# First transfers, products without a reader, row maxima on another engine and a 25th weight slot in a transformer layer with 32 experts

## The chip, the cores and the metric

The kernel runs on one core of one Trainium2 chip. The metric is the device time of one execution in microseconds (us): the median of the runs that are shown. The core has TensorE (PE in the profile; its weight loads are PEld), VectorE (DVE), ScalarE (ACT), GpSimd (POOL) and SyncE (SP), which here only issues transfers. The transfers themselves are carried by 16 DMA engines.

## What is computed

One transformer layer over 256 tokens of width 1024, in float32: attention in three branches (NSA), a gated recurrence (HGRN2), a merge, and 32 experts of which each token takes two.

```python
h = rmsnorm(x, attn_norm[layer])
proj = h @ w_in[layer]
...
mixed = (gate_nsa * (o_nsa.astype(x.dtype) @ w_br_nsa[layer]) +
         gate_hg * (o_hg @ w_br_hg[layer]))
x = x + mixed @ w_out[layer]
x = x + hier_moe(rmsnorm(x, ffn_norm[layer]), w_grp[layer], b_grp[layer], w_rtr[layer], b_rtr[layer],
                 w_gate[layer], w_up[layer], w_down[layer])
...
for e in range(N_EXPERTS):
    hid = jax.nn.silu(t @ w_gate[e]) * (t @ w_up[e])
    out = out + combine[:, e:e + 1] * (hid @ w_down[e]).astype(f32)
```

The expert weights are 32 x 6 pieces of 1 MB; the other weights are 30 blocks of about 1 MB.

## The kernel before

**The front** runs through the 30 blocks of `FRONT` in order: f0, f1, q0, q1, c0, ... m00, ... n1, and last o00, o10, o01, o11 (the product with `w_out`). `load_front` brings a block from HBM into a slot `raw`, on SP's queue. `split_part` (L273, L277) makes two parts of it: ACT writes `whi`, a copy in the reduced format fp32r, and DVE writes `wlo`, what is left. `three` (L410, L412, L413) then multiplies: four products with `whi`, and pairs of one with `wlo` and one with the low part of the other operand; twelve products are a group, four groups a block. For the first blocks the other operand is x^T, scaled by `attn_norm`, split by ACT (L369) and DVE (L371) into `hh_` and `hl_`. The side work of attention and recurrence runs between the groups.

**The slots.** Everything of 8 KB in a partition comes out of one pool of `WSLOTS` slots: raw blocks, `whi`, `wlo`, x, the merged activations `mh` (high parts) and `ml` (low parts), `h2T`, and the expert pieces `we`. A tile takes the slot that comes free first, and what fills it waits until the last reader of the slot's former content is done. `load_expert` (L308, L318) issues the expert pieces, in a fixed order and on SP's queue too: some during the front, by the table `EARLY` (a block's name and how many pieces behind its load), the others behind the front. SP issues in order, and has eight transfers under way at most.

**The routing** stands between o11 and the experts. PE makes the logits (L1024); `route(0)` and `route(1)` choose, for tokens 0 to 127 and 128 to 255, two experts each on DVE, down to a mask `mk` (L1055); `place` counts places with a product `ppos` (L1065) and DVE turns it into `mst` (L1068); `select_tile` makes the 0/1 matrix `lm` out of it (L1094); `gather_tile` gathers the tokens by products `pga` (L1103), which DVE scales into `xe` (L1113). Then the eight quads of four experts begin: `pg` and `pu` (L1207), then `py` (L1261). `residual` (L1121) puts x into the banks `acc`, to which the experts' output is added.

```python
    routed = route(0)
    ...
    with after(i):
        i = residual([0])
    ...
    i = placed[0]
    with after(i):
        i = gather_tile(0, 0, 0)
    i = place(1, i)
```

`after(i)` sets the order on an engine: what stands under it is issued behind i.

## Time and profile before

| | us |
|---|---|
| median of 3 runs | 694.04 |
| lowest, highest | 693.96, 695.82 |
| profiled execution, its own time | 695.66 |
| its span, first to last instruction | 693.9 |

The span is that of the profiled execution, and all times of rows count from its start. The front lies at 0 to 235, the routing at 235 to 247.6, the experts at 247.6 to 680, and the last sums and the store behind them. A view by windows lists, for each stretch, the busy time of each engine, the granted clock of TensorE as a share of 2.4 GHz, the busy share of the DMA engines and what they moved.

### The profile page before, as it was taken

The page shows a single profiled execution, that of the slowest core. Times are in us where ns is not written, and L with a number is a line of the kernel's source. Part 1 is how long each engine was busy: PE and PEld are TensorE (multiplying, and loading weights), DVE is VectorE, ACT ScalarE, POOL GpSimd, SP SyncE. Part 2 cuts the span into 40 slices and gives each one's busy share as a digit, 9 for nine tenths or more (in the row PEclk, how much of TensorE's full clock was granted, in tenths as well). Part 3 has the DMA queues.
Part 4 walks back from the last instruction along what each step waited for, and adds up shares of the span by engine and source line. Part 5 has one row for each costly group of instructions (what it writes and reads, how often), then busy time and mean ns, then how long its engine had stood idle before and what let it go on. Part 6 is the DMA issues. An engine that isn't in the chain of part 4 may idle for free. (4 is left out here: it accounts for less than half of the span.)

```text
span 693.9 us, 8708 instructions
## 1 busy us (share of the span) xinstructions
PE 569.3 (82%) x3628; PEld 318.0 (46%) x3628; DVE 211.4 (30%) x422; ACT 145.4 (21%) x231; POOL 37.3 (5%) x54
## 2 busy tenths in 40 slices
PE   5999999999999999988669668776865977795654
PEld 5988878887897754242123114221411421321111
DVE  5786656667557422121011002200200210110012
ACT  5433548474364210100000000000000000000002
POOL 0423302001000100000000000000000000000001
PEclk9999999999999989999899989988999897999896
DMA  8961533856646989999999999999999999999992
GB/s 321 418 241 65 179 122 148 334 192 232 255 177 248 376 340 421 421 422 419 423 419 422 422 420 421 421 422 420 422 419 422 420 421 422 421 422 419 408 360 89
DMA packets 39931, 238.84 MB, mean 344 GB/s; under 512 B 4176, under 2 KB 8784, under 8 KB 12752
## 3 DMA queue, kind: packets, MB, share of 16 engines
q1 hardware_dynamic: 39456, 237.70, 84.8%
q8 instruction: 30, 0.49, 0.3%
q10 hardware_dynamic: 432, 0.54, 0.2%
q14 instruction: 13, 0.11, 0.0%
HBM read 237.17 MB, written 1.05 MB: 343 GB/s over the span
## 5 line engine op out<-in xcount | busy, mean ns | idle before, releaser
L1207 PE MATMUL pu<-we,xe 128*32 128x512 f32 x512 | 99.2, 719 | 43.4 <-DMA we<-in_w_up 39.8
L1207 PE MATMUL pg<-we,xe 128*32 128x512 f32 x512 | 92.7, 669 | 34.8 <-DMA we<-in_w_gate 34.8
L1261 PE MATMUL py<-we,hT 128*32 128x512 f32 x448 | 74.3, 596 | 8.0 <-DMA we<-in_w_down 8.0
L1231 DVE SCALAR_TENSOR_TENSOR h<-pu,wv,h 128x512 f32<-128x512 f32 x8 | 8.7, 1089 | 234.0 <-PE pu L1207 234.0
L1207 PEld LDWEIGHTS pu<-we,xe 128*32 128x32 f32 x512 | 22.0, 127 | 116.1 <-DMA we<-in_w_up 70.1
L277 DVE TENSOR_TENSOR wlo<-raw,whi 128x2048 fp32r<-128x2048 f32 (+3 forms) x34 | 67.6, 1995 | 19.1 <-ACT whi L273 19.0
L1243 ACT ACTIVATE ys<-py,wv 128x512 fp32r<-128x512 f32 (+1 forms) x17 | 11.3, 663 | 268.0 <-PE py L1261 233.9
L1207 PEld LDWEIGHTS pg<-we,xe 128*32 128x32 f32 x512 | 20.1, 119 | 102.1 <-DMA we<-in_w_gate 64.8
L273 ACT ACTIVATE whi<-raw 128x2048 fp32r<-128x2048 f32 (+3 forms) x34 | 56.1, 1662 | 37.5 <-PE pxs L413 12.5
L412 PE MATMUL pws<-hl__94,whi 128*128 128x256 f32 x192 | 49.6, 289 | 0.0
L413 PE MATMUL pws<-hh__93,wlo 128*128 128x256 f32 x192 | 49.4, 288 | 0.0
L1261 PEld LDWEIGHTS py<-we,hT 128*32 128x32 f32 x448 | 20.4, 109 | 55.7 <-issue 33.7
L410 PE MATMUL pws<-hh__93,whi 128*128 128x256 f32 x192 | 33.9, 300 | 8.3 <-ACT hh__93 L369 8.3
L1244 DVE SCALAR_TENSOR_TENSOR ys<-py,wv,ys 128x512 fp32r<-128x512 f32 (+1 forms) x17 | 12.2, 718 | 89.5 <-ACT ys L1243 88.9
L412 PEld LDWEIGHTS pws<-hl__94,whi 128*128 128x128 f32 x192 | 37.8, 197 | 0.2 <-issue 0.2
L413 PEld LDWEIGHTS pws<-hh__93,wlo 128*128 128x128 f32 x192 | 37.9, 197 | 0.0
L1225 ACT ACTIVATE h<-pg,wv 128x512 f32<-128x512 f32 x8 | 9.2, 1147 | 131.8 <-PE pg L1207 131.8
L1103 PE MATMUL pga<-lm,x 128*128 128x128 f32 x256 | 32.7, 289 | 1.1 <-DVE lm L1094 1.1
L410 PEld LDWEIGHTS pws<-hh__93,whi 128*128 128x128 f32 x192 | 27.6, 197 | 11.2 <-ACT hh__93 L369 8.3
L1103 PEld LDWEIGHTS pga<-lm,x 128*128 128x128 f32 x256 | 31.7, 205 | 2.0 <-DVE lm L1094 2.0
L412 PE MATMUL pxs<-wlo,hh__93 128*128 128x512 f32 (+1 forms) x80 | 29.8, 376 | 0.0
L413 PE MATMUL pxs<-whi,hl__94 128*128 128x512 f32 (+1 forms) x80 | 29.5, 372 | 0.0
(241 smaller groups left out, 644.6 us busy)
## 6 DMA issues: line engine op xcount, KB each, us to landing
we<-in_w_gate SPq DMA_DIRECT2D x64, 1024.0 KB, 19.8
we<-in_w_up SPq DMA_DIRECT2D x64, 1024.0 KB, 19.8
we<-in_w_down SPq DMA_DIRECT2D x60, 1024.0 KB, 19.8
raw<-in_wf SPq DMA_DIRECT2D x27, 1024.0 KB, 4.9
we<-in_w_down SPq DMA_DIRECT2D x8, 512.0 KB, 10.6
raw<-in_wf SPq DMA_DIRECT2D x2, 560.0 KB, 9.9
raw<-in_wf SPq DMA_DIRECT2D x2, 512.0 KB, 6.5
xt__67<-in_xt SPq DMA_DIRECT2D x2, 512.0 KB, 6.9
```

The lines of the kernel that those rows point to most:

```text
L273: i = S.activation(his[n][:, c], raws[n][:, c], AF.Copy)
L277: splits.append((i, V.tensor_tensor(los[n][:, c], raws[n][:, c], his[n][:, c].bitcast(F32), op=OP.subtract)))
L410: PE.matmul(out_, lh, rh, start=start and i == 0, stop=False, skip_group_check=True)
L412: PE.matmul(out_, lh, rl, start=False, stop=False, skip_group_check=True)
L413: last = PE.matmul(out_, ll, rh, start=False, stop=stop and i == n - 1, skip_group_check=True)
L1103: i = PE.matmul(pgs[q, n][:, 128 * k:128 * k + 128], xv[:, tt, 512 * n + 128 * k:512 * n + 128 * k + 128], sel[q][:, tt], start=tt == 0 an ...
L1207: i = PE.matmul(p[32 * e:32 * e + 32], xes[q][:, 4 * hf + k, 32 * e:32 * e + 32], W[4 * q + e, hf][:, k], start=hf == 0 and k == 0, stop=h ...
L1225: S.activation(h, pg.rearrange("p (c j) -> p c j", j=4), AF.Silu, scale=r)
L1231: V.scalar_tensor_tensor(h, pu.rearrange("p (c j) -> p c j", j=4), r, h, op0=OP.mult, op1=OP.mult)
L1243: return (S.activation(hi[:, c], p[:, c], AF.Copy, scale=wv), V.scalar_tensor_tensor(lo[:, c], p[:, c], wv, hi[:, c].bitcast(F32), op0=OP. ...
L1244: V.scalar_tensor_tensor(lo[:, c], p[:, c], wv, hi[:, c].bitcast(F32), op0=OP.mult, op1=OP.subtract))
L1261: PE.matmul(py[n][32 * e:32 * e + 32], hTs[q][:, 2 * kh + j, 32 * e:32 * e + 32], WD[4 * q + e, kh][:, j, 512 * n:512 * n + 512], start=kh ...
```

## The change

- **First transfers.** Block f0 is stored as two halves that are each contiguous in HBM. x^T comes as `xa` (`attn_norm` and the first half), on ACT's queue, and `xb`, on SP's; before, both halves came on SP's queue behind the first half of f0. The vectors `vec` come in one transfer of 168 KB; before, 24 columns came first, on ACT's queue, and the others later.
- **Products without a reader.** 26 products of ones with ones (`WARM`; 128x256, bf16) stand ahead of PE's first product; nothing reads what they give.
- **Shift.** The eight multiplications of row maxima by -0.125 go from POOL (L808) to DVE.
- **Slots.** There are 25. The merged activations are kept by halves (`mT` 0 and 1, high and low part of a half in one slot), `h2T` goes to small tiles, and `EARLY` and the last count of `load_expert` add up to 25 pieces.
- **Routing.** `residual([0])` goes out of the routing into quad 0. In its place stand 16 products that nothing reads (`warm_up`; 128x128, bf16), 14 more behind the first `ppos` and 8 behind the second. The gather of the first 128 tokens is no longer cut by the second `ppos`. In `route(1)` the work of the first tile stands earlier.

```diff
+    blk[FRONT[0]] = blk[FRONT[0]].reshape(128, 2, -1).transpose(1, 0, 2)
...
+    vec = np.concatenate([pm(lb), pm(inp["ffn_norm"]), fin, pm(pos), pm(rt)], 1)
+    xt = rows128(np.ascontiguousarray(np.asarray(inp["x"])[0].T)).reshape(128, -1)
...
+        "xa": con(np.concatenate([an, xt[:, :1024]], 1)), "xb": con(xt[:, 1024:]), "wf": con(wf)[None], "wcmp": con(wc.reshape(128, -1)),
...
-WSLOTS = 24
+WSLOTS = 25
-STB = 1
+WARM = 26
-EARLY = {"h1": 3, "o00": 1, "m21": 1, "m00": 2, "o11": 1, "m01": 2, "m31": 2, "h0": 1, "o01": 1}
+EARLY = {"m20": 1, "h1": 3, "o00": 1, "m21": 1, "m00": 2, "o11": 2, "m01": 2, "m31": 2, "h0": 1, "o01": 2}
...
-    xt_ = slot("xt_")
-    xt8 = xt_.rearrange("p (k t) -> p k t", k=8)
+    xs = [slot(n) for n in ("xa", "xb")]
+    nc.scalar.dma_start(xs[0][:, :1032], xa)
+    an = xs[0][:, :8]
+    xt8 = [t.rearrange("p (k t) -> p k t", k=4) for t in (xs[0][:, 8:1032], xs[1][:, :1024])]
...
-    nc.scalar.dma_start(vc_[:, :24], vec[:, :24])
...
-                nc.sync.dma_start(raws[n][:, o:o + step], bass.AP(tensor=wf.tensor, offset=wf.offset + FOFF[n] + o,
-                                                                  ap=[[w, 128], [1, step]]))
+                nc.sync.dma_start(raws[n][:, o:o + step], bass.AP(tensor=wf.tensor, offset=wf.offset + FOFF[n] + 128 * o,
+                                                                  ap=[[step, 128], [1, step]]))
                 if n == FRONT[0] and o == 0:
-                    for c in range(0, 2048, 1024):
-                        nc.sync.dma_start(xt_[:, c:c + 1024], xt[:, c:c + 1024])
+                    nc.sync.dma_start(xs[1][:, :1024], xb)
...
+    nc.sync.dma_start(vc_, vec)
...
-    xn = slot("xn")
+
+    wz = mid.tile([128, 256], BF16, tag="xe", bufs=1, name="wz")
+    G.memset(wz, 1.0)
+    pw = bank("ns", "pw")
+    for _ in range(WARM):
+        PE.matmul(pw[:, :256], wz[:, :128], wz, start=True, stop=True)
...
-            last_hi = S.activation(hhi[:, k], xt8[:, k], AF.Copy, scale=an[:, k:k + 1])
+            last_hi = S.activation(hhi[:, k], xt8[q][:, k - 4 * q], AF.Copy, scale=an[:, k:k + 1])
         for k in ks:
-            last_lo = V.scalar_tensor_tensor(hlo[:, k], xt8[:, k], an[:, k:k + 1], hhi[:, k].bitcast(F32),
+            last_lo = V.scalar_tensor_tensor(hlo[:, k], xt8[q][:, k - 4 * q], an[:, k:k + 1], hhi[:, k].bitcast(F32),
...
-        G.tensor_scalar(mm[:, 1], mm[:, 0], -0.125, None, op0=OP.mult)
+        V.tensor_scalar(mm[:, 1], mm[:, 0], -0.125, None, op0=OP.mult)
...
-    def mk_mT():
-        return dict(hi=slot("mh", F32R).rearrange("p (k t) -> p k t", k=8),
-                    lo=slot("ml", F32R).rearrange("p (k t) -> p k t", k=8))
-
-    MT = Lazy(hi=mk_mT, lo=mk_mT)
+    def mk_mT(j):
+        def f():
+            t = slot("mT", F32R)
+            return {f"{n}{j}": a.rearrange("p (k t) -> p k t", k=4) for n, a in zip(("hi", "lo"), two(t))}
+        return f
+
+    MT = Lazy(hi0=mk_mT(0), lo0=mk_mT(0), hi1=mk_mT(1), lo1=mk_mT(1))
...
+                hi, lo = [getattr(MT, f"{n}{j}")[:, 2 * i:2 * i + 2] for n in ("hi", "lo")]
+                S.activation(hi, g, AF.Copy)
+                V.tensor_tensor(lo, g, hi.bitcast(F32), op=OP.subtract)
...
-    run(tokens_first("o00", MT.hi, MT.lo, accs[0], True, False, range(4)))
-    run(tokens_first("o10", MT.hi, MT.lo, accs[1], True, False, range(4)))
-
-
-    hT = slot("h2T")
-    h2T = hT.rearrange("p (t c) -> p t c", t=2)
+    run(tokens_first("o00", MT.hi0, MT.lo0, accs[0], True, False, range(4)))
+    run(tokens_first("o10", MT.hi0, MT.lo0, accs[1], True, False, range(4)))
+
+
+    h2T = {}
...
+        h2T[j, tt] = mid.tile([128, 512], F32, tag="ys", bufs=YSB, name="h2T")
...
-        V.tensor_reduce(gm, Gl, axis=AX.X, op=OP.max)
+        i = V.tensor_reduce(gm, Gl, axis=AX.X, op=OP.max)
+        with after(i):
+            between()
...
-        i = V.max(m8, EM)
-        with after(i):
-            between()
+        V.max(m8, EM)
...
-    run(tokens_first("o01", MT.hi, MT.lo, accs[0], False, True, range(4, 8), evac=resid(0)))
+    run(tokens_first("o01", MT.hi1, MT.lo1, accs[0], False, True, range(4), evac=resid(0)))
...
-    with after(i):
-        i = residual([0])
     pp = bank("ns", "ppos")
+
+    def warm_up(n, i):
+
+        with after(i):
+            for _ in range(n):
+                i = PE.matmul(acc[0][1][:, :128], before, before, start=True, stop=True, skip_group_check=True)
+        return i
+
+    i = warm_up(16, i)
 
     def first_tile():
         placed.append(place(0, i))
@@ -1136,13 +1153,14 @@
     placed = []
     with after(routed):
         route(1, first_tile)
-    i = placed[0]
+    i = warm_up(14, placed[0])
     with after(i):
-        i = gather_tile(0, 0, 0)
+        for n in range(2):
+            i = gather_tile(0, 0, n)
     i = place(1, i)
     select_tile(0, 1)
+    i = warm_up(8, i)
     with after(i):
-        gather_tile(0, 0, 1)
...
-        sT = mid.tile([128, 256], F32R, tag="sT", bufs=STB, name="sT")
+        sT = mid.tile([128, 256], F32R, tag="gs", bufs=GSB, name="sT")
...
-                residual([1, 2, 3])
+                residual(range(4))
...
-    load_expert(24 - sum(EARLY.values()))
+    load_expert(25 - sum(EARLY.values()))
```

How the rows of SP's queue change at the start (raw is a weight block's slot, vc holds `vec`, cs and cm constants). Before:

```order
L258 DMA raw<-in_wf 128x1024
L262 DMA xt__67<-in_xt 128x1024 x2
L258 DMA raw<-in_wf 128x1024
L258 DMA raw<-in_wf 128x2048
L330 DMA cs<-in_consts 128x202
L221 DMA x<-in_x 128x1024 x2
L258 DMA raw<-in_wf 128x2048
```

And now:

```order
L332 DMA vc__70<-in_vec 128x328
L261 DMA raw<-in_wf 128x1024
L264 DMA xb<-in_xb 128x1024
L261 DMA raw<-in_wf 128x1024
L261 DMA raw<-in_wf 128x2048
L333 DMA cs<-in_consts 128x202
L223 DMA x<-in_x 128x1024 x2
L261 DMA raw<-in_wf 128x2048
```

The vectors now stand ahead of the first half of f0, and the half of x^T that stood on this queue first has gone to ACT's.

PE's rows from the last logits to the first products of the experts (mk, lm, pga, ppos as above; pst turns `lm` round for later). Before:

```order
L1024 MATMUL prt<-vc__68,h2T 128x36 x4
L1121 MATMUL acc<-x_2028,cs 128x512
L1065 LDWEIGHTS before
L1065 MATMUL ppos<-mk,before 128x32
L1103 MATMUL pga<-lm,x_2028 128x128 x4
L1065 LDWEIGHTS before
L1065 MATMUL ppos<-mk,before 128x32
L1067 LDWEIGHTS ones
L1067 MATMUL ppos<-mk,ones 128x32
L1103 MATMUL pga<-lm,x_2028 128x128 x12
L1207 MATMUL pg<-we,xe 32x512 x32
```

And now (at each "..." the pair of rows ahead of it repeats: 16 pairs stand first, then 14, then 8):

```order
L1034 MATMUL prt<-vc__70,h2T 128x36 x4
L1144 LDWEIGHTS before
L1144 MATMUL acc<-before 128x128
...
L1075 MATMUL ppos<-mk,before 128x32
L1144 LDWEIGHTS before
...
L1113 MATMUL pga<-lm,x_2058 128x128 x8
L1077 MATMUL ppos<-mk,ones 128x32
...
L1201 MATMUL pst<-cs,lm 128x128
L1113 MATMUL pga<-lm,x_2058 128x128 x8
L1225 MATMUL pg<-we,xe 32x512 x32
```

The two products of `residual` are gone from here, 38 products of `warm_up` have come, and the gathers stand in two lots of equal size, the second tile's behind 8 of these. (A row counts an instruction of the program; the trace has two records for one of `pga`.)

DVE's rows in `route(1)`, behind the mask of the first tile. Before:

```order
L1055 TENSOR_SCALAR mk<-rt__2098 128x32
L1037 SCALAR_TENSOR_TENSOR rt__2098<-prt,rr,brow 128x36
L1043 TENSOR_REDUCE rt__2098<-rt__2098 128x1
L1044 SCALAR_TENSOR_TENSOR rt__2098<-rt__2098,cs 128x4
L1045 TENSOR_REDUCE rt__2098<-rt__2098 128x1
L1046 TENSOR_SCALAR rt__2098<-rt__2098 128x32
L1048 TENSOR_TENSOR rt__2098<-rt__2098 128x32
L1049 MAX rt__2098<-rt__2098 128x8
L1068 SCALAR_TENSOR_TENSOR mst<-ppos,mk 128x32
L1052 SCALAR_TENSOR_TENSOR rt__2098<-rt__2098,cs 128x32
L1094 TENSOR_TENSOR lm<-cs,mst 128x128
```

And now:

```order
L1065 TENSOR_SCALAR mk<-rt__2127 128x32
L1047 SCALAR_TENSOR_TENSOR rt__2127<-prt,rr,brow 128x36
L1053 TENSOR_REDUCE rt__2127<-rt__2127 128x1
L1078 SCALAR_TENSOR_TENSOR mst<-ppos,mk 128x32
L1056 SCALAR_TENSOR_TENSOR rt__2127<-rt__2127,cs 128x4
L1104 TENSOR_TENSOR lm<-cs,mst 128x128
L1057 TENSOR_REDUCE rt__2127<-rt__2127 128x1
L1058 TENSOR_SCALAR rt__2127<-rt__2127 128x32
```

The first tile's `mst` and `lm` stand five operations earlier in the second tile's chain.

## Rows read from the trace of the kernel before

**Rows 1.** Windows: length, busy engines (instructions), granted clock, DMA share, GB/s.

```profile
0.00:5.00 5.00, 0.00 (x0) 0.00 (x0) 0.00 (x0) 1.49 (x2) 0.36 (x7) 1.00 0.59 145
5.00:10.00 5.00, 1.74 (x5) 1.41 (x6) 3.22 (x8) 3.45 (x8) 0.00 (x0) 1.00 1.00 369
...
200.00:235.00 35.00, 34.02 (x201) 29.77 (x200) 19.48 (x21) 17.10 (x20) 1.20 (x4) 1.00 0.74 287
...
240.00:245.00 5.00, 3.89 (x20) 3.82 (x20) 2.08 (x11) 0.00 (x0) 0.00 (x0) 0.50 0.99 411
...
250.00:255.00 5.00, 5.00 (x49) 1.60 (x41) 0.51 (x4) 0.00 (x0) 0.00 (x0) 1.00 0.57 179
...
500.00:600.00 100.00, 72.59 (x387) 21.35 (x380) 7.70 (x18) 5.01 (x6) 0.00 (x0) 0.91 1.01 421
```

**Rows 2.** SP's timeline: start, us to the group's end, what was issued.

```profile
226.56 24.98 SPq L318 DMA_DIRECT2D we<-in_w_down  x8
...
260.21 17.72 SPq L308 DMA_DIRECT2D we<-in_w_up  x8
280.11 17.72 SPq L318 DMA_DIRECT2D we<-in_w_down  x8
```

**Rows 3.** Timeline of the routing, PE: start, us, operation, idle time and its releaser.

```profile
238.03 1.96 PE L1121 MATMUL acc<-x,cs 128*128 128x512 f32 x2
239.81 0.20 PE L1065 MATMUL ppos<-mk,before 128*128 128x32 bf16 x1
241.12 2.08 PE L1103 MATMUL pga<-lm,x 128*128 128x128 f32 x8 [1.11 <-DVE lm L1094]
...
243.09 4.55 PE L1103 MATMUL pga<-lm,x 128*128 128x128 f32 x24
247.57 4.93 PE L1207 MATMUL pg<-we,xe 128*32 128x512 f32 x44
```

**Rows 4.** Timeline of the routing, DVE.

```profile
238.76 0.24 DVE L1055 TENSOR_SCALAR mk<-rt__2098 128x32 bf16<-128x32 f32 x1
...
240.50 0.17 DVE L1068 SCALAR_TENSOR_TENSOR mst<-ppos,mk 128x32 f32<-128x32 f32 x1
...
240.78 0.28 DVE L1094 TENSOR_TENSOR lm<-cs,mst 128x128 f32<-128x128 f32 x1
```

**Rows 5.** Timeline of the start, PE and ACT.

```profile
8.26 1.78 PE L410 MATMUL pws<-hh__93,whi 128*128 128x256 f32 x4 [8.26 <-ACT hh__93 L369]
9.84 0.41 PE L412 MATMUL pws<-hl__94,whi 128*128 128x256 f32 x1
...
14.71 0.28 PE L412 MATMUL pws<-hl__94,whi 128*128 128x256 f32 x1
...
18.15 1.92 ACT L273 ACTIVATE whi<-raw 128x2048 fp32r<-128x2048 f32 x1 [2.28 <-DMA raw<-in_wf]
...
29.03 0.64 PE L410 MATMUL pws<-hh__93,whi 128*128 128x256 f32 x4
```

**Rows 6.** Timeline around the first o block, DVE and PE.

```profile
208.71 2.28 DVE L277 TENSOR_TENSOR wlo<-raw,whi 128x2048 fp32r<-128x2048 f32 x1
...
211.05 0.50 PE L412 MATMUL pwo<-wlo,mh 128*128 128x512 f32 x1 [0.98 <-DVE wlo L277]
```

**Rows 7.** Waits: who waited for whom, us in total, times, longest.

```profile
PE pno L863 <- ACT PT L844: 1.3, 1, 1.3
```

**Rows 8.** Windows in the expert stage, columns as in group 1.

```profile
470.00:475.00 5.00, 1.36 (x4) 0.14 (x2) 0.00 (x0) 0.00 (x0) 0.00 (x0) 1.00 1.01 416
475.00:482.00 7.00, 5.92 (x22) 1.17 (x26) 0.00 (x0) 0.00 (x0) 0.00 (x0) 0.51 1.02 424
```

**Rows 9.** Timeline of the last o block: SP's issue, ACT's split.

```profile
203.41 0.33 SPq L258 DMA_DIRECT2D raw<-in_wf  x1
...
218.91 1.92 ACT L273 ACTIVATE whi<-raw 128x2048 fp32r<-128x2048 f32 x1 [3.34 <-PE pwo L413]
```

**Rows 10.** The page, DMA issues: count, KB each, median us to landing.

```profile
raw<-in_wf SPq DMA_DIRECT2D x27, 1024.0 KB, 4.9
```

More of the change, by code (lines that the diff above doesn't have):

```diff
@@ L145, in _layout @@
     an, fin = [np.asarray(inp[k]).reshape(8, 128).T for k in ("attn_norm", "final_norm")]
-    vec = np.concatenate([an, pm(lb), pm(inp["ffn_norm"]), fin, pm(pos), pm(rt)], 1)
+    vec = np.concatenate([pm(lb), pm(inp["ffn_norm"]), fin, pm(pos), pm(rt)], 1)
+    xt = rows128(np.ascontiguousarray(np.asarray(inp["x"])[0].T)).reshape(128, -1)
     rows = np.concatenate([np.asarray(inp["hg_norm"])[0], np.asarray(inp["b_grp"])[0], np.asarray(inp["b_rtr"])[0]])[None]
@@ L155, in _layout @@
     }
-VEC = {"an": (0, 8), "lb": (8, 8), "fe": (16, 8), "fin": (24, 8), "pos": (32, 16), "rt": (48, 288)}
+VEC = {"lb": (0, 8), "fe": (8, 8), "fin": (16, 8), "pos": (24, 16), "rt": (40, 288)}
 ROWS = {"hgn": (0, 128), "br": (128, 36)}
@@ L177, in tile_block @@
 @with_exitstack
-def tile_block(ctx, tc, x, xp, xt, wf, wcmp, vec, rows, consts, lmask, w_gate, w_up, w_down, out, dbg=None, manual=False):
+def tile_block(ctx, tc, x, xp, xa, xb, wf, wcmp, vec, rows, consts, lmask, w_gate, w_up, w_down, out, dbg=None, manual=False):
     nc = tc.nc
@@ L333, in tile_block @@
     nc.sync.dma_start(cm_[:, :consts.shape[1] - kept], consts[:, kept:])
-    nc.sync.dma_start(vc_[:, 24:], vec[:, 24:])
     hgn = row("hgn", cm_[:, 384:])
@@ L375, in tile_block @@
     with after(second[1][0]):
-        sq = S.activation(xn[:, :1024], xv[:, 0], AF.Square, accum_out=st[:, 0:1])
+        sq = S.activation(xs[1][:, 1024:], xv[:, 0], AF.Square, accum_out=st[:, 0:1])
     with after(second[1][1]):
-        V.scalar_tensor_tensor(xn[:, 1024:], xv[:, 1], 1.0, xv[:, 1], op0=OP.mult, op1=OP.mult, accum_out=st[:, 1:2])
+        V.scalar_tensor_tensor(xs[0][:, :1024], xv[:, 1], 1.0, xv[:, 1], op0=OP.mult, op1=OP.mult, accum_out=st[:, 1:2])
     last_rx = rstd(rx, st[:, 0:2], D)
@@ L489, in tile_block @@
     lb, oml = lbt[:, 4:8], lbt[:, 8:12]
-    V.tensor_tensor(lbt[:, 0:4], ll[:, 0:4], ll[:, 4:8], op=OP.subtract)
+    with after(second[1][1]):
+        V.tensor_tensor(lbt[:, 0:4], ll[:, 0:4], ll[:, 4:8], op=OP.subtract)
     with after(sq):
@@ L1000, in squares @@
             q = 4 + 2 * j + tt
-            S.activation(h2T[:, tt, cs_] if not (j and tt) else sqs, xv[:, tt, cs_], AF.Square, scale=1 / 32,
+            S.activation(sqs, xv[:, tt, cs_], AF.Square, scale=1 / 32,
                          accum_out=st[:, q:q + 1])
@@ L1015, in x2_tr @@
         for c in [slice(0, 256), slice(256, 512)] if j and tt else [slice(0, 512)]:
-            last = S.copy(h2T[:, tt, 512 * j + c.start:512 * j + c.stop], p[:, c])
+            last = S.copy(h2T[j, tt][:, c], p[:, c])
         if j and tt:
@@ L1023, in logits @@
         for kk in range(4 * j, 4 * j + 4):
-            i = PE.matmul(pl[tt], h2T[:, tt, 128 * kk:128 * kk + 128], rt[:, kk],
+            i = PE.matmul(pl[tt], h2T[j, tt][:, 128 * kk - 512 * j:128 * kk - 512 * j + 128], rt[:, kk],
                           start=kk == 0, stop=kk == 7, skip_group_check=True)
@@ L1075, in tile_block @@
         later(logits, 0, tt)
-    run(tokens_first("o11", MT.hi, MT.lo, accs[1], False, True, range(4, 8), evac=resid(1),
+    run(tokens_first("o11", MT.hi1, MT.lo1, accs[1], False, True, range(4), evac=resid(1),
                      behind={(1, 2): lambda: x2_tr(1, 0)}), n=2)
```

4 lines of the change are left out of this document (removed).

## The prediction

> **What bounds the kernel now.** I read the windows first, for which resource is full in which stretch. Behind 255 us it is the DMA engines: in 500 to 600 us their share is 1.01 at 421 GB/s, while TensorE is busy for 72.59 of 100 us [rows 1]. So the expert stage goes at the pace of its weights. SP's timeline gives that pace: eight pieces of 1 MB begin at 260.21 and the next eight at 280.11, so one takes 19.90 / 8 = 2.49 us [rows 2]. A faster engine in there gains nothing.
>
> In 250 to 255 us, however, the DMA share is 0.57 at 179 GB/s [rows 1]. The transfers stand still there, and SP's timeline shows why: the group of eight that begins at 226.56 ends only at 226.56 + 24.98 = 251.54 [rows 2]. Its last piece waits for a slot. All 24 slots are taken (one by x, 23 by pieces), and the next comes free when `pg` has read the first piece of expert 0. `pg` begins at 247.57 [rows 3], and the issue follows 251.2 - 247.57 = 3.6 us later (the issue itself is the last 0.3 us of the group). From that moment on the rest is a fixed train: pieces left, times 2.49 us, and the last sums behind them. So the end moves by what that first release moves, and by 2.49 us for each piece that is loaded ahead of it in addition. This is the equation of all that follows.
>
> What sets the first release is TensorE's chain. In 200 to 235 us it is busy for 34.02 of 35 us [rows 1]; the front is bound by TensorE. The exceptions are what this change touches: its idle time until 8.26 us and the products at half the clock after it [rows 5], 0.98 us at the first o block [rows 6], 1.3 us at one wait in attention [rows 7], and the routing, where it waits 1.11 us for `lm` and then gathers at half the clock [rows 3].
>
> **The change part by part.**
>
> *The 25th slot.* The count of pieces ahead of the stop goes from 23 to 24: **2.49 us**. Is there room to load it? In 200 to 235 us the DMA engines are idle for 0.26 x 35 = 9.1 us [rows 1], and the halves of `mT` let the slots of half 0 go after o10 instead of after o11, so the pieces can use that time. The stop at 250 to 252 us is 2 us more of cover. If the piece did not land by then, it would be worth between 0 and 2.49 us; I see nothing that takes the cover away. `h2T` in small tiles and `sT` in another buffer add no transfer. The fourth `residual` product falls into quad 0, behind `pu`, ahead of a stage in which TensorE waits for weights: nothing.
>
> *Routing.* Now: `residual([0])` runs from 238.03 to 239.81, and only then `ppos` goes, though its mask was there at 238.76 + 0.24 = 239.00 [rows 3, 4]. `mst` starts at 240.50, behind five operations of `route(1)`; `lm` is ready at 241.06; the first 8 records of `pga` take 241.12 to 243.0, 0.23 us each, at a granted clock of 0.50 (1.2 GHz) [rows 1, 3, 4]; `pg` starts at 247.57. After: 16 short products in place of 1.8 us. Nothing of that shape is in the trace; the nearest is 128x256 at 0.12 us each at 2.4 GHz and 0.21 at 1.2 [rows 5], so I take 0.06 for half the columns at 2.4 GHz and 0.11 at 1.2. They end at 239.0 to 239.8, `ppos` at 239.3 to 240.0, and `lm` 0.17 + 0.28 and handovers behind it, at 239.9 to 240.6. But the next 14 stand ahead of the gather: 0.8 to 1.5 us. So the first gather begins at 240.1 to 241.5. From there three courses. If the clock stays at 2.4 GHz, 16 records at 0.11 us are 1.8 us, then the second `ppos`, `mst`, `lm` (0.9 us, with the 8 products under it), and 16 records again: `pg` at about 244.7, 2.9 us earlier. If it falls as now and comes back earlier, because the engine no longer pauses, some 10 of 32 records still run at 0.21 us: about 246.2, 1.4 us earlier. If it stays low until 246.5, as now, `pg` comes at 247.6 to 249.2, nothing won or 1.6 us lost. The clock was already falling while two dense products ran (238.03 to 239.99), so the first course is not the likeliest; I take the middle one, **1.4 us**, bounds -1.6 and 2.9.
>
> *Start.* The 26 products take 26 x 0.21 = 5.5 us at 1.2 GHz, in the 8.26 us in which TensorE has nothing to do [rows 5]; they cost nothing unless they start later than 2.7 us. Between 8.26 and 14.71 the single products go from 0.41 to 0.28 us in length, that is from 1.2 to 2.4 GHz [rows 5]. Three blocks of 48 products stand between 8.26 and 29.03, 20.8 us. At full clock, four products take 0.64 us of which the last is 0.28, so one takes 0.12 [rows 5], and 144 are 17.3 us: at most 3.5 us. It is not all kept. The split of q0 by ACT begins at 18.15 and waited 2.28 us for its transfer [rows 5]. ACT needs 1.92 us for it, DVE 2.28 for the low part [rows 5, 6], so `wlo` comes at 22.4; four of the products are done by then, and 44 x 0.12 = 5.3 us later, at 27.7, q0 is through: 1.3 us earlier than 29.03. The queue rows put `vec` ahead of f0: 168 KB, of which 12 KB came first before; 0.156 MB at 421 GB/s is 0.4 us, which leaves 0.9. Against that stand contiguous halves and the second queue. In the first 5 us the engines moved 145 GB/s, in the next 5 us 369 [rows 1]: 0.73 and 1.85 MB. The first 2 MB are the strided pieces, so most of those 369 GB/s are strided pieces too, and the slow start is rather of the time than of the stride. If contiguity cured it all, q0 would land up to 2 us earlier: 2.9 us. I take **1.3 us**, near the lower end, bounds 0.9 and 2.9 with the clock as hoped.
>
> A rule stands against the second queue. The Trainium skill ("DMA: Bandwidth & Descriptors", section "Issuing engines are not separate DMA queues") says that transfers of all issuing engines share the 16 DMA engines, so that several queues only save issue time. No run here has shown it yet; by it the second queue alone would leave the start term at the 0.9 us of the sum above.
>
> *First o block.* DVE's `wlo` for o00 starts one low part of `mT` (0.6 us) earlier in the new order, and TensorE waits 0.98 us for exactly that [rows 6]: **0.6 us**, bounds 0 and 0.98.
>
> *Shift.* Eight small operations go to DVE. Little in the front waits for them: TensorE's only wait at that place is 1.3 us for `PT` [rows 7]. So 0 to 1.3 us, and a loss of as much if DVE's queue delays another softmax; I take **0.3**.
>
> **Sum.** 2.5 + 1.4 + 1.3 + 0.6 + 0.3 = 6.1 us. The profiled execution took 695.66 us with a span of 693.9, 1.8 around it; it would come to 689.6. It lies 1.6 above the median of the runs, 694.04, and against the median the forecast is 694.04 - 6.1 = **687.9 us**.
>
> **Rivals.**
>
> *The clock falls again in front of q0.* With full clock TensorE ends f1 near 20 us and then has four products until 22.4. In the expert stage 1.36 busy of 5 us (470 to 475) were followed by 7 us at 0.51 [rows 8]. From 22.4 on at 0.21 us for each product, q0 would end at 30.6 if it stays low for those 7 us, and at 29.1 if for half of them. The start then loses 1.6 or gives nothing; with -0.5 the time is 694.04 - (6.1 - 1.8) = **689.7**. The warm-up that doesn't lift the clock at all ends here too. For it: the wait is real by the sum above. Against it: it is shorter than the 5 us of the row. The Trainium skill ("TensorE: Matmul & The Clock Gate", section "HAM oscillation — how this bites in real kernels") describes this course, short runs of products with waits for transfers between, each of which begins at the low clock again. The trace agrees in 470 to 482 us, where the clock fell behind such a wait; by the rule this rival's 689.7 would be the time.
>
> *Both halves go well.* Start 2.9 and routing 2.9: 2.5 + 2.9 + 2.9 + 0.6 + 0.3 = 9.2, **684.8**. One of the two alone gives 686.3 to 686.4.
>
> *The change does nothing.* All gains come before a stage that is bound by transfers, and they could vanish in it: **694.0**. Against it stands the stop at 250 us: were the engines full there, an earlier release would be worthless, but they are idle.
>
> *Slower.* SP issues in order, and the table now has one piece more behind m20, o01 and o11. A piece that waits for its slot holds back the raw block behind it. The last raw block is issued at 203.41 and split at 218.91 [rows 9]; 4.9 us of that is its transfer [rows 10], so 10 us are spare, and the block must come 10 + 6.1 = 16 us late before the kernel is slower, more than the time of two blocks. With 20 us it would be 694.04 + 3.9 = **698**. Most of the new pieces stand behind the last raw block, which speaks against it.
>
> **How the numbers follow.** The forecast's case has 0.50 (its own range 686.3 to 689.0, by the slips of the routing and the start), the clock in front of q0 0.25, both or one half going well 0.17, no effect 0.05, slower 0.03. The range from 684.8 to 690.7 leaves out no effect, slower, and the worst of the routing course (nothing or a loss there, together with a lost start). A change of 0.3%, 2.1 us, is about what a measurement of this kernel can tell from none. Faster by more than that: 0.92; within: 0.05; slower: 0.03.
>
> **What would show it.** In the trace after: 24 pieces issued ahead of the stop, and a stop that is still there; the train at 2.49 us a piece behind it, unchanged. `pg` at 244.0, that is 247.6 less the four terms ahead of it (1.4 + 1.3 + 0.6 + 0.3 = 3.6). The first product near 8.3 us at 0.28 us in length, q1's first product at 27.7. A first product later than 9 us would show that `vec` ahead of f0 costs more than I think; lengths of 0.41 us in q0 the clock's fall; a gather at 0.23 us to the end the worst course of the routing. The prediction is wrong if the stop is gone (then the slots' order is not what I read), or if the pace behind it differs.

## The result and the profile after

The changed kernel takes 686.81 us (median of 4 runs, 686.17 to 687.95), the kernel before on the same chip 694.0; the ratio is 0.9893, 95% interval 0.9874 to 0.9912. That is 7.2 us less, where 6.1 were forecast (687.9), inside the range. On a difference of two such medians the interval is some 1.3 us wide to either side, so the times alone cannot tell less than that. The profiled execution took 686.17 us, the fastest of the four, with a span of 684.2.

The windows of the changed kernel, columns as in [rows 1]:

```profile
0.00:5.00 5.00, 3.86 (x19) 2.67 (x20) 0.00 (x0) 1.49 (x2) 0.61 (x8) 1.00 0.64 225
...
15.00:20.00 5.00, 5.00 (x44) 5.00 (x43) 2.73 (x7) 2.01 (x2) 0.90 (x2) 1.00 0.81 311
...
240.00:245.00 5.00, 5.00 (x51) 1.89 (x53) 3.48 (x23) 0.86 (x6) 0.00 (x0) 1.00 0.47 193
...
500.00:600.00 100.00, 74.31 (x396) 23.54 (x388) 8.09 (x15) 3.64 (x4) 0.00 (x0) 0.88 1.01 420
```

Read against [rows 1]: the first 5 us move 225 GB/s, not 145; the stop of the transfers has gone from 250 to 255 us to 240 to 245; the expert stage is as full as it was, at 420 GB/s for 421. In 15 to 20 us there is a hole (share 0.81 at 311 GB/s) that the prediction did not foresee. The same window of the kernel before has none:

```profile
15.00:20.00 5.00, 5.00 (x44) 5.00 (x44) 2.89 (x7) 2.72 (x4) 0.90 (x2) 1.00 1.04 399
```

SP's timeline of the changed kernel at the stop, and its last groups:

```profile
217.50 14.95 SPq L320 DMA_DIRECT2D we<-in_w_down  x8
244.25 5.24 SPq L310 DMA_DIRECT2D we<-in_w_gate  x8
...
611.27 17.80 SPq L310 DMA_DIRECT2D we<-in_w_up  x8
631.23 33.09 SPq L324 DMA_DIRECT2D we<-in_w_down  x12
```

The last groups of the kernel before:

```profile
619.67 17.72 SPq L308 DMA_DIRECT2D we<-in_w_up  x8
639.55 32.97 SPq L322 DMA_DIRECT2D we<-in_w_down  x12
```

24 pieces are now issued ahead of the stop, and the 25th waits until 244.25, where the 24th waited until 251.21 in [rows 2]. From the release to the end of the span it is 684.2 - 244.25 = 439.95 us; before it was 693.9 - 251.21 = 442.69, one piece of 2.49 more and 0.25. That looks as if nothing else had changed, but two differences cancel in it. A group of eight pieces now takes 631.23 - 611.27 = 19.96 us, before 639.55 - 619.67 = 19.88: over the 168 pieces behind the release the train loses some 1.3 us. And from SP's last issue to the end it is 684.2 - 664.32 = 19.88 us, before 693.9 - 672.52 = 21.38: the end gains 1.5. The experiments below narrow down the first; what makes the second, none of them isolates.

The routing on PE, which answers to [rows 3]:

```profile
230.98 0.39 PE L419 MATMUL pwo<-whi,mT 128*128 128x512 f32 x1
...
234.03 1.06 PE L1144 MATMUL acc<-before 128*128 128x128 bf16 x16
235.06 0.19 PE L1075 MATMUL ppos<-mk,before 128*128 128x32 bf16 x1
235.10 0.94 PE L1144 MATMUL acc<-before 128*128 128x128 bf16 x14
235.91 2.05 PE L1113 MATMUL pga<-lm,x 128*128 128x128 f32 x16
...
238.62 2.05 PE L1113 MATMUL pga<-lm,x 128*128 128x128 f32 x16
240.60 7.07 PE L1225 MATMUL pg<-we,xe 128*32 128x512 f32 x64
```

The last product of o11 in the kernel before:

```profile
234.98 0.39 PE L413 MATMUL pwo<-whi,ml 128*128 128x512 f32 x1
```

Sixteen records of `pga` take 2.05 us, where eight took 2.08. The clock stays at 2.4 GHz (1.00 in 240 to 245, where before had 0.50). The last o block ends at 231.37, before at 235.37, so `pg` comes 9.23 us behind it instead of 12.20: 3.0 us, as in the best course of the prediction.

The start on PE and ACT, which answers to [rows 5]; the last two rows are the split of q1 and the first product of the block behind it, c0:

```profile
1.14 5.58 PE L368 MATMUL pw<-wz 128*128 128x256 bf16 x26 [1.14 <-POOL ones L403]
...
7.58 1.59 PE L416 MATMUL pws<-hh__93,whi 128*128 128x256 f32 x4 [0.86 <-ACT hh__93 L375]
...
16.73 1.91 ACT L275 ACTIVATE whi<-raw 128x2048 fp32r<-128x2048 f32 x1 [2.34 <-DMA raw<-in_wf]
...
23.39 2.94 ACT L275 ACTIVATE whi<-raw 128x2048 fp32r<-128x2048 f32 x2 [0.54 <-DMA raw<-in_wf]
...
32.95 0.42 PE L416 MATMUL pxs<-whi,hh__93 128*128 128x280 f32 x2
```

The products begin at full clock and 0.7 us earlier, q0's split 1.4 us earlier. But the same row of c0 stands at 34.79 before, only 1.8 us later:

```profile
34.79 0.42 PE L410 MATMUL pxs<-whi,hh__93 128*128 128x280 f32 x2
```

And no other profile with this order of transfers has c0 so early, as the experiments show.

### The profile page after: what moved, and what is told of

Read it like the earlier page. It is cut to its first block, busy times and chain, and to the rows that moved or that the text cites. A ratio compares the mean times of both kernels' runs of the same rounds, so it can differ in the third digit from the quotient of the medians.

```text
span 684.2 us, 8830 instructions
## 1 busy us (share of the span) xinstructions
PE 576.8 (84%) x3692; PEld 317.8 (46%) x3692; DVE 212.1 (31%) x430; ACT 145.2 (21%) x231; POOL 32.5 (5%) x47
## 3 DMA queue, kind: packets, MB, share of 16 engines
q10 hardware_dynamic: 432, 1.05, 0.4%
HBM read 237.17 MB, written 1.05 MB: 348 GB/s over the span
## 5 line engine op out<-in xcount | busy, mean ns | idle before, releaser
L1225 PE MATMUL pg<-we,xe 128*32 128x512 f32 x512 | 95.4, 689 | 35.2 <-DMA we<-in_w_gate 35.2
L1279 PE MATMUL py<-we,hT 128*32 128x512 f32 x448 | 76.2, 596 | 9.4 <-DMA we<-in_w_down 9.3
L418 PE MATMUL pws<-hl__94,whi 128*128 128x256 f32 x192 | 48.5, 284 | 0.0
L1279 PEld LDWEIGHTS py<-we,hT 128*32 128x32 f32 x448 | 19.8, 109 | 59.6 <-issue 35.5
L418 PEld LDWEIGHTS pws<-hl__94,whi 128*128 128x128 f32 x192 | 36.7, 191 | 0.2 <-issue 0.2
L416 PE MATMUL pws<-hh__93,whi 128*128 128x256 f32 x192 | 33.3, 293 | 0.9 <-ACT hh__93 L375 0.9
L1113 PE MATMUL pga<-lm,x 128*128 128x128 f32 x256 | 30.3, 276 | 0.0
L1113 PEld LDWEIGHTS pga<-lm,x 128*128 128x128 f32 x256 | 29.3, 192 | 0.2 <-DVE lm L1104 0.2
L416 PEld LDWEIGHTS pws<-hh__93,whi 128*128 128x128 f32 x192 | 26.6, 191 | 4.7 <-issue 1.9
```

What stands on the lines that cost most here:

```text
L416: PE.matmul(out_, lh, rh, start=start and i == 0, stop=False, skip_group_check=True)
L418: PE.matmul(out_, lh, rl, start=False, stop=False, skip_group_check=True)
L1113: i = PE.matmul(pgs[q, n][:, 128 * k:128 * k + 128], xv[:, tt, 512 * n + 128 * k:512 * n + 128 * k + 128], sel[q][:, tt], start=tt == 0 an ...
L1225: i = PE.matmul(p[32 * e:32 * e + 32], xes[q][:, 4 * hf + k, 32 * e:32 * e + 32], W[4 * q + e, hf][:, k], start=hf == 0 and k == 0, stop=h ...
L1279: PE.matmul(py[n][32 * e:32 * e + 32], hTs[q][:, 2 * kh + j, 32 * e:32 * e + 32], WD[4 * q + e, kh][:, j, 512 * n:512 * n + 512], start=kh ...
```

## Experiments

Each kernel changes one thing of the changed kernel, unless said otherwise. Each is compared with the kernel before on the same chip as well; that kernel's medians on the four chips differ by up to 1.2 us. Distances inside a profile (from one row to another) repeat far better than the times, so the verdicts rest on these.

**The kernel before, once more.** 

> The kernel before, once more with a profile. The two profiled executions differ by 9.7 us in span (693.9 and 684.2), the medians only by 7.2. Theory: the stages ahead of the experts are the same in each execution but for the clock, which falls at other moments; so the first product of q1 stands at 29.0, the first of o00 at 209.0, and only pg moves, to 245 to 247.6, by a shorter stretch at 1.2 GHz in the routing. Rival: the stages are fixed to 0.2 us (pg at 247.6 again) and the 2 us lie in the train of expert pieces, whose pace was 2.486 us a piece in one and 2.494 in the other execution.

Its own time is 694.38 us, its span 692.6. From its timeline, PE:

```profile
242.41 4.07 PE L1103 MATMUL pga<-lm,x 128*128 128x128 f32 x24
246.41 5.79 PE L1207 MATMUL pg<-we,xe 128*32 128x512 f32 x52
```

c0 begins at 34.04, o00 at 208.28, o11 ends at 234.68, and `pg` comes 11.73 us behind that, not 12.20. So the theory holds in kind, though it had put all of the difference into the routing: 0.75 us come from the start, where the clock rose earlier, and 0.47 from the routing. The blocks between them repeat to 0.1 us. Release to end is 442.5 against 442.7, and a group of eight pieces takes 19.88 us in both: the pace of the train belongs to the kernel and not to the execution.

**The shift back on POOL.**

```diff
-        V.tensor_scalar(mm[:, 1], mm[:, 0], -0.125, None, op0=OP.mult)
+        G.tensor_scalar(mm[:, 1], mm[:, 0], -0.125, None, op0=OP.mult)
```

> The changed kernel with the eight multiplications back on POOL. Theory: in block m00 POOL's operation takes 2.2 us again because it runs beside DVE's wlo, ACT's copy PT stands behind it, and m00 takes 1.6 us longer (from 11.6 to 13.2); all later stages and the end move by 1.6, to about 688.4. Rival (the forecast's term): 0.3 us, to 687.1, and the 1.6 us of m00 come from other operations that changed place.

688.39 us (4 runs), 6.1 below the kernel before on its chip, where the changed kernel gained 7.2. Its timeline in block m00:

```profile
168.53 2.29 DVE L279 TENSOR_TENSOR wlo<-raw,whi 128x2048 fp32r<-128x2048 f32 x1
...
168.69 2.20 POOL L815 TENSOR_SCALAR mst<-mst 128x4 f32<-128x4 f32 x1 [7.71 <-DVE mst L812]
170.92 0.51 ACT L819 ACTIVATE Ps<-Ps,mst 128x256 f32<-128x256 f32 x1 [4.31 <-POOL mst L815]
...
172.91 0.57 ACT L851 ACTIVATE PT<-pnt 128x512 f32<-128x512 f32 x1
...
173.53 1.62 PE L870 MATMUL pno<-PT,nq 128*64 128x128 f32 x16 [1.31 <-ACT PT L851]
```

This is the chain of [rows 7] again. POOL's multiplication of 512 numbers takes 2.20 us, beside a `wlo` of 2.29 on DVE that began 0.16 us ahead of it; ACT waits 4.31 us for it, and the copy `PT`, which needs nothing of it, stands behind four `Ps` on ACT. In the changed kernel the same chain reads:

```profile
169.71 0.60 ACT L851 ACTIVATE PT<-pnt 128x512 f32<-128x512 f32 x1 [3.83 <-PE pnt L847]
169.99 0.16 DVE L815 TENSOR_SCALAR mst<-mst 128x4 f32<-128x4 f32 x1
...
171.41 1.09 PE L870 MATMUL pno<-PT,nq 128*64 128x128 f32 x16
```

On DVE it takes 0.16 us, and `PT` has moved ahead of the four `Ps`. m00's and m01's first products, in the kernel before and then in the changed one:

```profile
164.94 0.72 PE L410 MATMUL pws<-hh__93,whi 128*128 128x256 f32 x4
...
178.89 0.74 PE L410 MATMUL pws<-hh__93,whi 128*128 128x256 f32 x4
```

```profile
163.19 0.72 PE L416 MATMUL pws<-hh__93,whi 128*128 128x256 f32 x4
...
175.50 0.74 PE L416 MATMUL pws<-hh__93,whi 128*128 128x256 f32 x4
```

From one to the other it is 13.95 us before (13.97 in the second profile of before, 13.97 here with POOL) and 12.31 in the changed kernel: 1.64 us. The theory holds; the change's gain in time is 1.1 to 1.6.

**24 slots.**

```diff
-WSLOTS = 25
+WSLOTS = 24
...
-EARLY = {"m20": 1, "h1": 3, "o00": 1, "m21": 1, "m00": 2, "o11": 2, "m01": 2, "m31": 2, "h0": 1, "o01": 2}
+EARLY = {"h1": 3, "o00": 1, "m21": 1, "m00": 2, "o11": 2, "m01": 2, "m31": 2, "h0": 1, "o01": 2}
...
-    load_expert(25 - sum(EARLY.values()))
+    load_expert(24 - sum(EARLY.values()))
```

> The changed kernel with 24 slots (the piece behind m20 taken out of the table, 24 in the last count). Theory: 23 pieces ahead of the stop, pg unchanged at 240.6, the end 2.5 us later, about 689.3. Rival: the half tiles of mT alone free the slots early enough, or the DMA engines' start from the stop hides a piece, and the loss is under 1 us.

689.71 us, 4.8 below the kernel before: 2.4 to 2.9 of the gain are lost. Its SP timeline at the stop:

```profile
218.83 26.60 SPq L320 DMA_DIRECT2D we<-in_w_down  x8
245.52 4.83 SPq L310 DMA_DIRECT2D we<-in_w_gate  x7
```

The 24th piece waits again, until 245.1; from there to the end are 442.3 us, against 439.95. `pg` came 9.23 us behind o11 as in the changed kernel. One slot is one piece.

**The routing of before.**

```diff
-    i = warm_up(16, i)
+    with after(i):
+        i = residual([0])
...
-    i = warm_up(14, placed[0])
+    i = placed[0]
     with after(i):
-        for n in range(2):
-            i = gather_tile(0, 0, n)
+        i = gather_tile(0, 0, 0)
```

(also without `warm_up(8)`, with the second part of the first tile's gather behind the second `ppos`, with `between` behind the maximum, and `residual([1, 2, 3])` in quad 0). 

> The changed kernel with the routing of before (residual([0]) in place, no warm_up, the gathers and the first tile's mst and lm in their old order). Theory: the clock falls to 1.2 GHz at the gathers again and pg comes 3.0 us later, at 243.6, the end at about 689.8. Rival: the fall of before was a matter of the moment; pg comes 0.5 to 1.5 us later only, from the order.

689.56 us, 4.9 below the kernel before: 2.3 to 2.75 of the gain are lost. Its PE timeline:

```profile
238.94 2.07 PE L1113 MATMUL pga<-lm,x 128*128 128x128 f32 x8 [1.11 <-DVE lm L1104]
...
240.91 4.29 PE L1113 MATMUL pga<-lm,x 128*128 128x128 f32 x24
245.13 7.07 PE L1225 MATMUL pg<-we,xe 128*32 128x512 f32 x64
```

o11 ends at 233.19, `pg` is 11.94 us behind. In all three profiles with the old routing the clock fell to 1.2 GHz ahead of the gathers: the granted clock is 0.92 in 238 to 240 us and 0.50 behind it in the first profile of before, 0.50 from 238 on in the second, and here 0.74 in 236 to 238 and then 0.50. Each time it fell while the two products of `residual` ran, or right behind them.

**The new order without the 38 products.**

```diff
-    i = warm_up(16, i)
...
-    i = warm_up(14, placed[0])
+    i = placed[0]
...
-    i = warm_up(8, i)
```

> The changed kernel without the 38 products in the routing; residual([0]) in quad 0 and the new order of gathers and of lm stay. Theory: without them TensorE falls to 1.2 GHz as before, ppos goes at 0.1 us behind its mask, the first 16 gathers take 0.2 us each and pg comes about 2 us later behind the end of o11 than the 9.23 us of the changed kernel (11.0 to 11.5; 11.9 to 12.2 with the old routing); the time is 688.4 to 689. Rival: the order alone gives the gain (pg at 9.5 to 10 us behind o11), the products cost as much as they give, and the time stays within 0.7 us of 686.8.

688.04 us, 6.6 below the kernel before; neither the theory (688.4 to 689) nor the rival (up to 687.5) had this time. In the profile the theory fell. PE's rows, and a window:

```profile
236.66 0.19 PE L1075 MATMUL ppos<-mk,before 128*128 128x32 bf16 x1 [0.85 <-DVE mk L1065]
237.51 2.05 PE L1113 MATMUL pga<-lm,x 128*128 128x128 f32 x16 [0.66 <-DVE lm L1104]
...
242.19 7.07 PE L1223 MATMUL pg<-we,xe 128*32 128x512 f32 x64
```

```profile
236.00:238.00 2.00, 0.68 (x5) 0.59 (x6) 1.83 (x11) 0.00 (x0) 0.51 (x1) 1.00 1.00 418
```

o11 ends at 232.97 and `pg` is 9.22 us behind, the changed kernel's 9.23, with TensorE busy for 0.68 of 2 us and the clock at 1.00. In this execution the products gave nothing and cost nothing: the order alone did it. From o11's end to the first gather it is 5.75 us with the old order and 4.54 with the new one, with products or without; from there to `pg` it is 5.97 to 6.45 with the old order and 4.68 to 4.69 with the new one. So 1.2 us come from the work ahead of the gathers and 1.3 to 1.8 from the gathers themselves, which no longer run at half the clock.

c0 began at 34.62 in this profile, 1.7 us later than in that of the changed kernel, and that is all by which the spans differ (685.9 and 684.2). The median of its six runs, however, is 1.2 us above that of the changed kernel, and 1.5 and 1.8 above those of two kernels with the 38 products on the same chip (the whole start of before, and 36 products with late small transfers, below). Whether the clock falls in some of these runs, so that the products pay as an insurance, one profile does not tell.

**No products at the start** (`WARM = 0`). 

> The changed kernel without the 26 products ahead of the first one. In three of four profiles of kernels with these products TensorE was at 1.2 GHz again soon after its first real product, and in all of them the first product of c0 came at 33.0 to 34.8 us, against 34.0 and 34.8 before, because q1's transfer landed late. Theory: c0 is held by q1's transfer, so without the products c0 starts at 34 to 34.8 and the time rises by less than 0.7 us over 686.8. Rival (the forecast's term): the products are what gives the start, and the time rises by 1.3 us or more.

687.13 us, 6.3 below the kernel before. c0 begins at 33.76. The time is in the theory's range and the rival fell, but not for the theory's reason: q1's split waits for no transfer here.

**36 products** (`WARM = 36`). 

> 36 products in place of 26, so that they reach to the first real one and no pause is left ahead of it. Theory: TensorE stays at 2.4 GHz from the first real product on (0.28 us each), q0 starts at 20.4 to 20.6, but c0 comes at 33 to 34 as before, and the time falls by 0 to 0.7 us. Rival: the clock falls all the same, or the products delay the first real one by over 0.5 us, and nothing or a loss comes of it.

686.8 us, 6.6 below the kernel before; q0 at 20.37, c0 at 33.47. The real products run at full clock from the first on (four in 1.41 us at 7.69, then 0.28 each). The theory holds in the profile; the time does not fall.

Of the seven profiles with 26 products, four have the clock at 1.2 GHz again between the first real product and some 12 us (24 slots, shift on POOL, old routing, and f0 as before, below), three have not; none of the three with 36 has. TensorE has nothing to do between the end of the 26 products and the first real one, at 7.3 to 8.3. With f0 contiguous, f1's first product then stands at 15.4 to 15.9 or at 14.4; without products it is 16.1. But c0 does not follow. ACT's split of q1 and PE's first product of c0, kernel by kernel:

| kernel | q1's split | c0 | apart |
|---|---|---|---|
| before, two profiles | 25.21, 24.46 | 34.79, 34.04 | 9.58, 9.58 |
| changed | 23.39 | 32.95 | 9.56 |
| 24 slots | 24.20 | 33.75 | 9.55 |
| shift on POOL | 24.21 | 33.77 | 9.56 |
| routing of before | 25.20 | 34.75 | 9.55 |
| 36 products | 23.92 | 33.47 | 9.55 |
| no products | 24.18 | 33.76 | 9.58 |

c0 comes 9.55 to 9.58 us behind the split of q1 whatever TensorE's clock was. In four of the six kernels with the new start (changed, 24 slots, routing of before, 36 products) the split waits for q1's transfer, 0.3 to 1.6 us; there the transfer holds c0. In the other two, and in the kernel before, the split waits for TensorE's own third last group, and the products then run on with hardly a pause (1.44 us a group). The distance is the same there, but what holds c0 is TensorE.

**f0 as before.**

```diff
-    blk[FRONT[0]] = blk[FRONT[0]].reshape(128, 2, -1).transpose(1, 0, 2)
-                nc.sync.dma_start(raws[n][:, o:o + step], bass.AP(tensor=wf.tensor, offset=wf.offset + FOFF[n] + 128 * o,
-                                                                  ap=[[step, 128], [1, step]]))
+                nc.sync.dma_start(raws[n][:, o:o + step], bass.AP(tensor=wf.tensor, offset=wf.offset + FOFF[n] + o,
+                                                                  ap=[[w, 128], [1, step]]))
```

> The changed kernel with f0 stored as before (each half with a stride). The first 5 us moved 225 GB/s with contiguous halves and 145 before. Theory: the contiguous halves make this, so the first split of f0 comes about 1 us later (7.0 instead of 6.0), the first product at 8.3 or later, and q0's transfer lands at 18 again; the time stays within 0.5 us, because c0 is set by q1's transfer. Rival: the start of the queue is slow whatever the stride, the second queue made the difference, and the first split stays at 6.0.

688.0 us, 5.4 below the kernel before: 1.2 to 1.8 us of the gain are lost, more than either side said. Its first window:

```profile
0.00:5.00 5.00, 3.86 (x19) 2.75 (x20) 0.00 (x0) 1.49 (x2) 0.61 (x8) 1.00 0.62 208
```

The first split of f0 goes from 5.98 to 6.66 (5.70 to 6.22 in the other profiles with contiguous halves), the first product from 7.58 to 8.26, q1's split to 25.99 and c0 to 35.54. Neither side had it: the stride costs some 0.7 us at f0, but 208 of the 225 GB/s are there without contiguous halves of f0, from the second queue, from x^T, which is contiguous too, or from the vectors in one transfer. Which of these, no run tells apart.

**Three small transfers later.**

```diff
-    nc.sync.dma_start(cm_[:, :consts.shape[1] - kept], consts[:, kept:])
-    hgn = row("hgn", cm_[:, 384:])
-    brow = row("br", cp.tile([128, 36], F32, name="brow"))
...
-    nc.sync.dma_start(wcm, wcmp)
+    with after(nc.sync.dma_start(wcm, wcmp)):
+        nc.sync.dma_start(cm_[:, :consts.shape[1] - kept], consts[:, kept:])
+        hgn = row("hgn", cm_[:, 384:])
+        brow = row("br", cp.tile([128, 36], F32, name="brow"))
```

> The changed kernel with three small transfers (cm, 192 KB, and two of rows, 64 and 18 KB) put behind q1, c0 and wcm on SP's queue. In the changed kernel the DMA engines are only 0.57 to 0.8 busy between 16 and 19 us, when these are served, and q1 lands at 23.3 to 25.1 us. Theory: they make that hole; without them ahead q1 lands at about 21.5 to 22, c0's first product comes at 32 to 33, and the time falls by 0.8 to 1.5 us to about 685.7. Rival: the hole comes from something else (lanes, the number of transfers under way), stays where it is, and the time stays within 0.5 us.

686.4 us, 7.0 below the kernel before. The window of the hole and the one behind it, and q1's split on ACT:

```profile
15.00:20.00 5.00, 5.00 (x44) 5.00 (x43) 2.74 (x7) 2.01 (x2) 2.62 (x4) 1.00 1.01 410
20.00:25.00 5.00, 4.71 (x38) 4.46 (x37) 3.72 (x6) 2.37 (x3) 3.23 (x4) 1.00 0.91 356
```

```profile
23.16 2.92 ACT L276 ACTIVATE whi<-raw 128x2048 fp32r<-128x2048 f32 x2
```

The hole is gone from 15 to 20 us (0.81 to 1.01) and has moved with the three transfers: 20 to 25 us has 0.91 at 356 GB/s and 25 to 30 us 0.87 at 355, where the changed kernel has 1.02 in both. q1's split waits for no transfer any more: it waits for the end of the third last group of products, which the code asks for. c0 comes at 32.70, the earliest of the profiles so far. That these transfers make the hole and that it held q1 is shown; the time fell by 0.4 us, less than the theory's 0.8 to 1.5 and less than the runs can tell. They do not make it by themselves: in the kernel before the same three stand ahead of q1 too, and 15 to 20 us has 1.04 at 399 GB/s.

**The whole start of before** (with f0, x^T, vectors and products as there; slots, shift and routing as changed). 

> The changed kernel with the whole start of before: f0 strided, x^T on SP's queue, the vectors in two transfers, no products ahead of the first; slots, shift and routing as changed. Theory: the start's real worth is what c0's first product moves, 34.0 and 34.8 before against 33.0 to 33.8 in most profiles of the changed start, so 0.7 us, and the time is about 687.5. Rival (the forecast's term): 1.3 us or more, 688.1 and above. Third: nothing or less, 686.8 or below, since the strided f0 with the other changes gave 688.0.

686.5 us (5 runs, 685.83 to 686.75), 8.1 below the kernel before; ratio 0.9884, interval 0.9865 to 0.9902. The third case holds: all that was done to the start is worth nothing that these runs can tell from zero. In its profile c0 begins at 34.44; the five with the new start and 26 products in the same order of transfers have 33.0 to 34.75, 34.0 on the mean, so perhaps 0.4 us.

The profile shows where these go. From the release (245.69) to the end it is 438.81 us; the ten other kernels with 24 pieces ahead have 439.74 to 440.10. Its last groups:

```profile
611.62 17.74 SPq L308 DMA_DIRECT2D we<-in_w_up  x8
631.51 32.91 SPq L322 DMA_DIRECT2D we<-in_w_down  x12
```

A group of eight takes 19.89 us, as in the kernel before; in all eleven kernels with the new start, or most of it, most groups take 19.94 to 19.96. So the new start lets the train begin earlier and makes it slower, and the two cancel. It is also why f0 as before, with a late c0 and the slow train, lost time that the whole start of before did not lose. Which part slows the train is not shown. It is slow without the products at the start, with f0 as before and with late small transfers; left are x^T on two queues, the vectors in one transfer, and what goes with these.

**36 products and late small transfers together.** 

> The changed kernel with 36 products at the start and the three small transfers behind wcm. Theory: the two do not add up, because q1's split then waits for the third last group of products (23.2 us in the run with late small transfers), so c0 starts at 32.6 to 32.9 in every execution; the time is 685.8 to 686.4. Rival: c0 comes below 32.3 and the time at 685.5 or less.

686.27 us, 8.3 below the kernel before, which is the theory's time, but not by its way: c0 came at 33.68, later than with either of the two alone (33.47 and 32.70). The timeline of DVE and POOL at q0 shows why:

```profile
19.27 1.04 POOL L403 CAST lm<-lmf 128x1024 uint8<-128x1024 f32 x1 [1.67 <-DMA lmf<-in_lmask]
19.28 1.05 DVE L501 TENSOR_SCALAR lbt<-lbt 128x4 f32<-128x4 f32 x1 [1.16 <-ACT lbt L500]
20.25 2.28 DVE L280 TENSOR_TENSOR wlo<-raw,whi 128x2048 fp32r<-128x2048 f32 x1
...
22.58 0.39 PE L420 MATMUL pws<-hh__89,wlo 128*128 128x256 f32 x1 [1.32 <-DVE wlo L280]
```

With the mask `lmf` earlier, POOL's cast of 1.04 us falls beside a DVE operation on 512 numbers, which takes 1.05 us (0.17 in the changed kernel); q0's `wlo` starts that much later, and PE waits 1.32 us.

**The same with the split free after the fourth last group** (`HOLD = 4`). 

> The same, and a split may begin when the fourth last group of products has ended, not the third last. Theory: q1's split begins at 21.7 instead of 23.2, TensorE no longer waits 0.5 us for q1's low part, c0 starts at 32.1 to 32.3, and the time is about 0.5 us lower than with three, 685.4 to 685.9. Rival: the earlier splits stand ahead of other work on ACT and DVE in the rest of the front, and the gain is lost or turns into a loss of up to 1 us.

687.82 us, 6.8 below the kernel before, 1.55 above the one with three. c0 came at 32.64, but m00 at 165.09, 132.45 us behind, where it is 130.2 in the kernel before and the changed one: the rival, and more of it than it said. Between the two TensorE's waits for DVE grow from 1.7 to 3.6 us.

No version here beats the changed kernel clearly. The best medians are 686.27, 686.4 and 686.5, up to half a microsecond under it, less than the runs tell apart.

## Why the prediction came out as it did

The equation was right: the end is the first release, plus the pieces left at 2.49 us each, plus the last sums. From release to end it is 442.5 and 442.7 with 23 pieces ahead, 442.3 with 24 slots, and 438.8 to 440.1 with 24 pieces ahead. But I took the pace and the last sums for constants, and neither is. The pace went from 19.88 / 8 = 2.485 to 19.95 / 8 = 2.494 us with the new start, which costs some 1.3 us; a pace that differs was one of my signs of being wrong. From SP's last issue to the end it is 21.4 and 21.5 us in the two profiles of before and 19.8 to 20.1 in the twelve others, which gives 1.5 us for a reason that no run isolates. That the two cancel is luck.

- *25th slot, 2.5 us.* Right: 2.35 us by the trains, 2.4 to 2.9 by the times.
- *Routing, 1.4 us.* The place was right, the size too small: 2.5 to 3.0 in the profiles, 2.3 to 2.75 in the times. The step that failed is the choice between the three courses. I took the middle one because the clock was already falling under two dense products; in each of eleven profiles with the new order the gathers ran at 2.4 GHz. The products in the gaps, on which I hung this, did not show to be the cause: without them `pg` stands at the same distance. Why the clock fell with the old order and not with the new one, though TensorE was busy for less, is not settled; the nearest difference, the two products of `residual` during which it fell, was not tried by itself.
- *Start, 1.3 us.* Wrong: perhaps 0.4 at c0, and nothing in the time (the kernel with the whole old start is 0.3 us faster by the medians, 0.9 by the gains over the kernel before). Three links failed. I put the pinch at q0 and its transfer; that came 1.4 us earlier and no longer held anything in the changed profile, where q1's first product stands at 26.44, ahead of the 27.7 that I gave. The pinch went on to q1, whose transfer came late behind the hole at 15 to 20 us. The rival of the falling clock came, but in f0's products rather than in front of q0, in four of seven profiles; in three of the four (24 slots, routing of before, f0 as before) the split of q1 waited for its transfer in any case. And the train became slower with the new start, which the term left out.
- *First o block, 0.6 us.* Right: from o00's to o10's first product it is 6.74 before and 6.13 after.
- *Shift, 0.3 us, bounds 0 to 1.3.* Wrong in size: 1.64, outside the bound. The bound came from the one wait of 1.3 us on PE in [rows 7]. It held no longer when ACT's order changed as well: PE gained the wait and 0.3 us of products that had stood apart. What made the wait I had not looked at, a POOL operation ten times as long as its seven sisters.

The sum of the measured terms is 2.4 + 2.7 + 0.4 + 0.6 + 1.6 = 7.7, less 1.3 for the pace and 1.5 more at the end 7.9, against 7.2 between the medians (interval 6.1 to 8.7). Routing and shift came out 1.3 us above their terms each, the start 0.9 below, the train 1.3 below and the end 1.5 above; that the forecast is only 1.1 us off is in good part luck. The slower rival (SP's order) did not come: the raw blocks landed in time. The rival of no effect fell by the 24 slots and the routing.

## What to carry to other kernels

Where a stage runs at the pace of its transfers, find the moment that starts the train and count what is loaded ahead of it; each microsecond of the chain up to that moment and each piece ahead of it are worth their full time, and no faster engine in the stage is. Compare the pace of the train as well, to the third digit: 0.3% of it was worth 1.3 us here, as much as the whole start was forecast to give. A gain at the start of a chain is worth what the next late thing leaves of it, so follow it to the block behind, here from f0 to q0 to q1. And look at the one long operation among short sisters: it was worth more than the most elaborate part of the change.
